# State space preparation in two feed forwards instead of three, modulation sums one stage later, low parts of weights back on VectorE

## The chip, the cores and the metric

The kernel runs on one core of one Trainium2 chip. The metric is the device time of one execution in microseconds (us). The profile is one execution of the same program, seen by the hardware profiler: TensorE (PE, with its weight loads as PEld), VectorE (DVE), ScalarE (ACT), GpSimd (POOL), and SyncE (SP), which issues the transfers.

## The reference, cut to what matters

Two blocks of two layers run one after the other on 256 latent rows and 256 context rows of width 1024. Every layer has a half feed forward, a mixer and another half feed forward, each one modulated by shift, scale and gate vectors that come from a condition vector. The mixers are a convolution module and a neighbourhood attention in the first block, a joint attention and an S5 state space mixer in the second.

```python
def second_block(x, c, ctx, c_ctx, mod_w, mod_b, ...):
    for l in range(DEPTH):
        m_lat = jnp.moveaxis((jax.nn.silu(c) @ mod_w[l] + mod_b[l]).reshape(b, N_MOD, 1, D_MODEL), 1, 0)
        h_lat = ffn_sublayer(h_lat, m_lat, 0, norm_pre[l, 0], norm_post[l, 0], ffn_w13[l, 0], ffn_w2[l, 0])
...
def s5_discretise(lam_re, lam_im, b_re, b_im, log_step):
    dt = jnp.exp(log_step)[:, None]
    mag = jnp.exp(lam_re * dt)
    a_re = mag * jnp.cos(lam_im * dt)
    a_im = mag * jnp.sin(lam_im * dt)
...
    bb_re = f_re[..., None] * b_re - f_im[..., None] * b_im
    bb_im = f_re[..., None] * b_im + f_im[..., None] * b_re
```

Nothing of `s5_discretise` depends on `x`, nor do the modulation vectors: both can be worked out at any time before their use. The outputs are float32.

## The kernel before, in words

**Matmuls.** All large products are made in pieces: each float32 operand is split into a high part, rounded for the matmul, and a low part, the rest. A product takes three matmuls (high by high, low by high, high by low). Activations lie transposed, 128 features on the partitions, in `hh` and `hl` (high and low): columns 0 to 255 are the latent stream, 256 to 511 the context stream.

**Weights.** `plan` lists all weight chunks in order. `pump` loads a chunk (`raw`, at most 1 MB, three buffers) from SP's queue, and for each piece of 8 tiles of 128 by 128 ScalarE writes the high part `wh` (L181) and another engine subtracts it for the low part `wl` (L186); five pieces are kept ahead. Which engine makes the low part is set by `cvm`: with 0 it is always VectorE, with 2 every second piece goes to GpSimd. `cvm` is 0 in the feed forwards with both streams (until the last products of one) and in the convolution, and 2 elsewhere. While `cv_behind` is set (during the convolution's layer norm) all go to GpSimd.

**Stages.** The order in time, with the names used here: f100, conv, f102, f110, na (neighbourhood attention), f112, f200, attn, f202, f210, s5, f212. A name f*bln* is the feed forward of block *b*, layer *l*, sublayer *n*. All run on both streams but f112 and f212, which have the latent one alone. A feed forward takes 22 gate and up tiles (`gu`) in three groups of 6, 8 and 8, and after each group the 8 down tiles (`pd`). Behind each `gu` pair VectorE multiplies (L778), ScalarE writes the high part `Hh` (L780), VectorE the low part `Hl` (L781).

**Side work.** The program is written in the order of TensorE's instructions, with a planner's clock `pe_t` that each matmul moves on by its cost (216 ns for 512 columns). A `Task` is a generator that takes a step whenever that clock passes its due time; a step that yields a number is followed by a pause of at least that many ns. Two tasks run inside the feed forwards. Each engine's own order follows from the program's order and from when the scheduler of the program takes an instruction to be ready.

- `mods` makes the modulation vectors on VectorE: each 128 of the 9216 outputs of a layer are one multiply and sum `jk` (L536) of a 512 KB weight tile `mw` with the condition vector, for one stream or both. Its period spreads the sums over 0.84 of a feed forward with both streams (0.8 of one with one stream). `open_mw` opens the buffers of `mw`, three by default.
- `s5_pre` works out the tables of the state space mixer. First constants on 64 columns (powers on GpSimd, sine and cosine on ScalarE, the rest on VectorE); then 8 groups, each with small powers on VectorE (`pn`, `pw`), `bb`, inputs `vw`, outputs `ow` and rotations `E` on GpSimd, 16 transposes `pvt` and 16 small products `kp` on TensorE, and transfers to DRAM (`dV`, `dO`, `dE`, `dK`). At the end of a group `toeplitz` reads `dK` back in a new order (`tt`) and stores `dT`. A step is due every 1500 ns (`PRE_STEP`). The task runs in f100, f102 and f110 and is drained after f110. All its buffers are in one pool, open from the start until after f110.

**Sums by stage before.** f100: 112 (from column group 16 on of layer (1,0), and the rest of that layer); f102: 48 of layer (1,1); f110: 64 of (1,1) and 48 of (2,0); f112: 48 of (2,0); f200: 48 of (2,0) and 48 of (2,1); f202: 64 of (2,1).

## Time and profile before

| | us |
|---|---|
| three runs, median | 3692.72 |
| three runs, lowest and highest | 3685.61 and 3693.66 |
| the profiled execution | 3693.2 |
| its span, first to last instruction | 3691.4 |
| TensorE matmuls, busy | 3497.5 (95% of the span) |
| TensorE weight loads, busy | 3058.1 (83%) |
| VectorE busy | 2641.6 (72%) |
| ScalarE busy | 1380.8 (37%) |
| GpSimd busy | 1199.6 (32%) |

Busy time is a mean over stages that differ, so the stages have to be read one by one. Matmuls are pipelined and their ends are modelled, so TensorE's busy time is not its peak rate. Times in the rows below count from the span's start.

### The profile page before, as it was taken

To read this page: it belongs to the slowest core of one execution; us is meant where nothing else is said; L and a number is where in the kernel's file an instruction comes from. 1 tells how busy PE (TensorE), PEld (TensorE's weight loads), DVE (VectorE), ACT (ScalarE), POOL (GpSimd) and SP (SyncE) were. 2 spreads that over 40 slices of the span, in tenths; PEclk is the share of its full clock that TensorE was granted. 3 is DMA by queue.
4 is the path that set the end of the run, shared out by engine and by line. 5 is a ranking of instruction groups with operands and counts; after the bars stand their busy time and mean duration, and the time that the engine had idled before them with its cause. 6 is when DMAs were issued, how large, how long until landed. Compare 5 with 4: busy or idle time off the path is not lost. (4 is left out here: it accounts for less than half of the span.)

```text
span 3691.4 us, 54762 instructions
## 1 busy us (share of the span) xinstructions
PE 3497.5 (95%) x21160; PEld 3058.1 (83%) x21160; DVE 2641.6 (72%) x4360; ACT 1380.8 (37%) x2430; POOL 1199.6 (32%) x1021
## 2 busy tenths in 40 slices
PE   8989999999999999999999998899999999997898
PEld 7768867988887788888998888778888988885898
DVE  8998798866589886778987766877565733368633
ACT  4222444422232223554343224555322432233443
POOL 5667301655564641123420004323000300035343
PEclk9999999999999999999999999999999999998899
DMA  7565311455447763235755542104455332238353
GB/s 255 174 219 201 131 69 41 166 171 186 158 147 261 266 212 123 101 115 184 258 197 198 183 145 93 45 31 142 166 198 172 139 113 103 92 115 286 123 186 126
DMA packets 158125, 580.41 MB, mean 157 GB/s; under 512 B 25252, under 2 KB 56740, under 8 KB 118184
## 3 DMA queue, kind: packets, MB, share of 16 engines
q1 hardware_dynamic: 157864, 576.91, 44.8%
q8 instruction: 166, 2.72, 0.3%
q14 instruction: 95, 0.78, 0.1%
HBM read 547.55 MB, written 29.29 MB: 156 GB/s over the span
## 5 line engine op out<-in xcount | busy, mean ns | idle before, releaser
L181 ACT ACTIVATE wh<-raw 128x1024 fp32r<-128x1024 f32 (+1 forms) x679 | 700.5, 1038 | 1353.3 <-PE gu L107 725.0
L107 PE MATMUL gu<-hl,wh 128*128 128x512 f32 (+1 forms) x3136 | 1084.0, 347 | 4.3 <-DVE hl L694 3.3
L107 PE MATMUL gu<-hh,wl 128*128 128x512 f32 (+1 forms) x3136 | 1082.5, 346 | 4.8 <-DVE wl L186 4.6
L107 PE MATMUL gu<-hh,wh 128*128 128x512 f32 (+1 forms) x3136 | 1078.4, 348 | 8.3 <-ACT hh L691 7.8
L186 DVE TENSOR_TENSOR wl<-raw,wh 128x1024 fp32r<-128x1024 f32 (+1 forms) x544 | 706.8, 1302 | 367.7 <-ACT wh L181 360.1
L186 POOL TENSOR_TENSOR wl<-raw,wh 128x1024 fp32r<-128x1024 f32 (+1 forms) x135 | 344.3, 2553 | 1278.4 <-ACT wh L181 1216.3
L536 DVE CUSTOM_DVE_ANT_0 jk<-mw,cb,vec 128x1024 bf16<-128x1024 f32 x480 | 704.8, 1468 | 50.8 <-DMA mw<-in_mw_dram 39.2
L107 PEld LDWEIGHTS gu<-hl,wh 128*128 128x128 f32 x3136 | 600.1, 191 | 77.6 <-DVE hl L694 4.8
L107 PEld LDWEIGHTS gu<-hh,wh 128*128 128x128 f32 x3136 | 597.5, 192 | 80.4 <-ACT hh L691 9.4
L107 PEld LDWEIGHTS gu<-hh,wl 128*128 128x128 f32 x3136 | 600.2, 192 | 76.9 <-DVE wl L186 5.9
L107 PE MATMUL pd<-Hh,wh 128*128 128x256 f32 (+1 forms) x1696 | 565.8, 335 | 19.3 <-ACT Hh L780 17.5
L107 PE MATMUL pd<-Hl,wh 128*128 128x256 f32 (+1 forms) x1696 | 567.8, 335 | 9.6 <-DVE Hl L781 9.6
L107 PE MATMUL pd<-Hh,wl 128*128 128x256 f32 (+1 forms) x1696 | 567.0, 335 | 0.0
L107 PEld LDWEIGHTS pd<-Hh,wh 128*128 128x128 f32 x1696 | 325.6, 192 | 52.9 <-ACT Hh L780 19.8
L107 PEld LDWEIGHTS pd<-Hl,wh 128*128 128x128 f32 x1696 | 326.2, 192 | 42.7 <-DVE Hl L781 11.7
L107 PEld LDWEIGHTS pd<-Hh,wl 128*128 128x128 f32 x1696 | 326.1, 192 | 30.4 <-issue 0.2
L778 DVE TENSOR_TENSOR gu<-sg,gu 128x512 f32<-128x512 f32 (+1 forms) x196 | 113.2, 578 | 203.6 <-PE gu L107 196.5
L107 PE MATMUL pj<-hh,wh 128*128 128x256 f32 (+1 forms) x736 | 226.5, 323 | 10.7 <-ACT hh L691 7.5
L107 PE MATMUL pj<-hl,wh 128*128 128x256 f32 (+1 forms) x736 | 227.7, 314 | 1.7 <-DVE hl L1089 1.0
L107 PE MATMUL pj<-hh,wl 128*128 128x256 f32 (+1 forms) x736 | 227.3, 314 | 0.8 <-DVE wl L186 0.8
L780 ACT ACTIVATE Hh<-gu 128x512 fp32r<-128x512 f32 (+1 forms) x196 | 98.6, 503 | 346.0 <-DVE gu L778 345.8
L107 PEld LDWEIGHTS pj<-hh,wh 128*128 128x128 f32 x736 | 142.5, 201 | 21.2 <-ACT hh L691 8.7
(403 smaller groups left out, 4602.0 us busy)
## 6 DMA issues: line engine op xcount, KB each, us to landing
raw<-in_gu_dram SPq DMA_DIRECT2D x186, 1024.0 KB, 4.8
mw<-in_mw_dram SPq DMA_DIRECT2D x280, 512.0 KB, 4.1
raw<-in_dn2b_dram SPq DMA_DIRECT2D x38, 1024.0 KB, 4.7
raw<-in_dn1b_dram SPq DMA_DIRECT2D x32, 1024.0 KB, 6.0
raw<-in_dn1a_dram SPq DMA_DIRECT2D x16, 768.0 KB, 4.4
raw<-in_pw_dram SPq DMA_DIRECT2D x12, 1024.0 KB, 4.8
raw<-in_dn2a_dram SPq DMA_DIRECT2D x16, 768.0 KB, 4.2
dO<-ow SPq DMA_DIRECT2D x32, 256.0 KB, 2.7
```

Source lines behind the costliest of these rows:

```text
L107: ins = self.last_mm = self.nc.tensor.matmul(out=out, lhsT=lhsT, rhs=rhs, start=start, stop=stop, **kw)
L181: ins = nc.scalar.activation(out=h2, in_=r, func=AF.Copy)
L186: self.low_p = lambda eng=eng, l2=l2, r=r, h2=h2: eng.tensor_sub(l2, r, h2.bitcast(F32))
L536: self.behind_pe(nc.vector.tensor_tensor_reduce(out=jk, in0=tl[i], in1=self.cb[s], scale=1.0, scalar=self.V(f"mod_b{b}{l}")[:, j:j + 1], o ...
L778: nc.vector.tensor_mul(pr[:, :n], sg[:, :n], pu[:, :n])
L780: nc.scalar.activation(out=hi, in_=pr[:, :n], func=AF.Copy)
```

## The change: what it does

- `s5_pre` takes a pause of its own after the constants (`yield "pause"`: the task is taken off the list). It starts again in f102, and only then is the pool for the buffers of the groups opened (`s5w`, through `work`). The 8 groups run in f102 and f110.
- `toeplitz` of a group no longer follows it with pauses of 4000 and 5000 ns: it is kept as `back`, and its four chunks are issued one by one between the parts of the next group (`next(back, None)`). Only behind the last group it runs by itself. Both halves share one buffer `tt`.
- The modulation sums of (2,0) column group 0 move from f110 to f112, those of group 1 from f112 to f200, those of (2,1) group 0 from f200 to f202. In f112 they come ahead of the norm of the context stream (`ctx_norm`). f110 no longer loads the second block's condition vectors. Sums by stage: f100 112, f102 48, f110 64, f112 48, f200 96, f202 112.
- f102 and f110 have two `mw` buffers instead of three.
- `cvm` is gone: low parts of weights are made on VectorE everywhere, but for the time in which `cv_behind` is set.

```diff
@@ -69,7 +69,9 @@
     def step(self):
         r = next(self.gen, "end")
         self.done = r == "end"
-        if not self.done:
+        if r == "pause":
+            self.k.stop(self)
+        elif not self.done:
             self.t = max(self.t + self.period, self.k.pe_t + max(r or 0, 0.5 * self.period))
 
 
@@ -82,7 +84,7 @@
         self.chains = []
         self.ticking = False
         self.tasks = []
-        self.cvm, self.cv_behind = 2, None
+        self.cv_behind = None
         P = lambda name, bufs, **kw: ctx.enter_context(tc.tile_pool(name=name, bufs=bufs, **kw))
         self.pool = lambda name, bufs=1, side="left": tc.tile_pool(name=name, bufs=bufs, side=side, reuse_waits="tile")
         self.const = P("const", 1)
@@ -181,7 +183,7 @@
             ins = nc.scalar.activation(out=h2, in_=r, func=AF.Copy)
             if self.cv_behind:
                 self.behind(ins, self.cv_behind)
-            eng = nc.gpsimd if (self.cvm and self.n_cv % self.cvm == 1) or self.cv_behind else nc.vector
+            eng = nc.gpsimd if self.cv_behind else nc.vector
             self.low()
             self.low_p = lambda eng=eng, l2=l2, r=r, h2=h2: eng.tensor_sub(l2, r, h2.bitcast(F32))
             self.cv_t[self.n_cv] = (hi, lo)
@@ -719,7 +721,6 @@
         nc, tc = self.nc, self.tc
         two = len(streams) == 2
         N = 512 if two else T
-        self.cvm = 0 if two else 2
         with ExitStack() as es:
             Hh = Hl = fp = None
 
@@ -855,7 +856,6 @@
                         self.drain(task)
                     if side is not None:
                         self.stop(side)
-                    self.cvm = 2
                 if full < KT:
                     ws = {}
                     for s in streams:
@@ -1092,7 +1092,6 @@
                 self.rstd(ch, acc, 2, 1e-5, apply, d1=0, d2=0)
                 rdy[s] = ch
 
-            self.cvm = 0
             w0 = [self.take() for _ in range(2)]
             for s in S2:
                 self.force(ready[s])
@@ -1131,7 +1130,6 @@
             self.release(2 * L)
             go()
             self.cv_behind = None
-            self.cvm = 2
             mean(KT - 1, CTX)
             layernorm(CTX)
             self.cv_behind = None
@@ -1855,7 +1853,7 @@
         self.dT = [t(f"dT{d}", [128, 1024]) for d in range(8)]
         self.dU = [t(f"dU{d}", [128, 512]) for d in range(8)]
 
-    def s5_pre(self, sp):
+    def s5_pre(self, sp, work):
 
         nc = self.nc
         g, v, a = nc.gpsimd, nc.vector, nc.scalar
@@ -1944,6 +1942,8 @@
         v.tensor_mul(fi, fi, den)
         yield
         three = lambda t: t.rearrange("p (d q) -> p d q", d=2)
+        yield "pause"
+        sp = work()
         bbz = [sp.tile([128, 2, 4, 32], F32, name=f"bbz{i}") for i in range(2)]
         for t in bbz:
             g.memset(t, 0.0)
@@ -1965,15 +1965,16 @@
         def toeplitz(d):
 
             for hf in range(2):
-                tt = sp.tile([128, 4, 128], F32, tag=f"vt{hf}", name="tt")
+                tt = sp.tile([128, 4, 128], F32, tag="tt", name="tt")
                 src = self.dK[d].rearrange("(g h) e -> h g e", h=16)
                 for j in range(8):
                     nc.sync.dma_start(out=tt[16 * j:16 * j + 16], in_=src[:, 4 * hf:4 * hf + 4, 16 * j:16 * j + 128])
-                yield 5000
+                yield
                 nc.sync.dma_start(out=self.dT[d][:, 512 * hf:512 * hf + 512].rearrange("p (g e) -> p g e", g=4), in_=tt)
-                yield 4000
+                yield
 
         ahead = load(0)
+        back = iter(())
         for d in range(8):
             bc = ahead
             if d < 7:
@@ -2130,11 +2131,15 @@
                                           in_=t[:, 4 * r:4 * r + 4, :].rearrange("p q e -> p (q e)"))
 
 
+            next(back, None)
             V1 = yield from inputs(1)
+            next(back, None)
             O1 = yield from outputs(1)
             yield from turned(1, V1)
+            next(back, None)
             V0 = yield from inputs(0, lambda: store_outputs(1, O1))
             yield from steps(1, O1)
+            next(back, None)
             O0 = yield from outputs(0)
             yield from turned(0, V0)
             E = yield from rotations()
@@ -2142,8 +2147,10 @@
             yield from steps(0, O0)
             store_rotations(E)
             nc.sync.dma_start(out=self.dK[d], in_=kt)
-            yield 4000
-            yield from toeplitz(d)
+            back = toeplitz(d)
+        yield 4000
+        for _ in back:
+            yield 5000
 
     def plan_s5(self):
         for p in range(4):
@@ -2389,8 +2396,8 @@
         self.plan_s5()
         self.plan_ffn(2, 1, 1)
 
-        with self.pool("s5p", 1, "right") as sp:
-            pre = Task(self, self.s5_pre(sp), PRE_STEP)
+        with self.pool("s5p", 1, "right") as sp, ExitStack() as late:
+            pre = Task(self, self.s5_pre(sp, lambda: late.enter_context(self.pool("s5w", 1, "right"))), PRE_STEP)
             self.open_mw(None)
             begin = self.begin
             self.mark("f100")
@@ -2401,20 +2408,15 @@
             self.close_mw()
             self.mark("conv")
             self.conv(ready, gates(1, 0, 1), lambda s, acc: norm(1, 0, 2, s, acc))
-            self.open_mw(["c", "c_ctx"])
+            self.open_mw(["c", "c_ctx"], 2)
             self.mark("f102")
             self.ffn(1, S2, ready, gates(1, 0, 2), lambda s, acc: norm(1, 1, 0, s, acc),
                      work=self.mods(mods(1, 1, [0], 40)), side=pre, **ht("102"))
             self.close_mw()
-            self.open_mw(["c", "c_ctx"])
+            self.open_mw(["c", "c_ctx"], 2)
             self.mark("f110")
-
-            def two_mods():
-                yield from self.mods(mods(1, 1, [1, 2], 40))[0]
-                self.c_names = ["c_2", "c_ctx_2"]
-                yield from self.mods(mods(2, 0, [0]))[0]
             self.ffn(1, S2, ready, gates(1, 1, 0), lambda s, acc: norm(1, 1, 1, s, acc),
-                     work=(two_mods(), 116), side=pre, **ht("110"))
+                     work=self.mods(mods(1, 1, [1, 2], 40)), side=pre, **ht("110"))
             self.close_mw()
             self.drain(pre)
         self.mark("na")
@@ -2454,23 +2456,23 @@
         self.mark("f112")
 
         def norm_and_mods():
+            yield from self.mods(mods(2, 0, [0]))[0]
             yield from ctx_norm()
-            yield from self.mods(mods(2, 0, [1]))[0]
-        self.ffn(1, (LAT,), ready, gates(1, 1, 2, (LAT,)), final, work=(norm_and_mods(), 58))
+        self.ffn(1, (LAT,), ready, gates(1, 1, 2, (LAT,)), final, work=(norm_and_mods(), 61))
         self.close_mw()
 
         self.open_y()
         self.open_mw(["c_2", "c_ctx_2"])
         self.mark("f200")
         self.ffn(2, (CTX, LAT), ready, gates(2, 0, 0), after2(2, 0, 0, (2, 0, 1)),
-                 work=self.mods(mods(2, 0, [2]) + mods(2, 1, [0])), **ht("00"))
+                 work=self.mods(mods(2, 0, [1, 2])), **ht("00"))
         self.close_mw()
         self.mark("attn")
         self.attn2(ready, after2(2, 0, 1, (2, 0, 2)))
         self.open_mw(["c_2", "c_ctx_2"])
         self.mark("f202")
         self.ffn(2, S2, ready, gates(2, 0, 2), after2(2, 0, 2, (2, 1, 0)),
-                 work=self.mods(mods(2, 1, [1, 2], 40)), **ht("02"))
+                 work=self.mods(mods(2, 1, [0]) + mods(2, 1, [1, 2], 40)), **ht("02"))
         self.close_mw()
         tabs = self.es.enter_context(self.pool("s5t"))
         self.s5_tab = {}
```

## Rows read from the trace of the kernel before

**Rows 1.** The page: busy time of each engine, share of the span, instructions.

```profile
PE 3497.5 (95%) x21160; PEld 3058.1 (83%) x21160; DVE 2641.6 (72%) x4360; ACT 1380.8 (37%) x2430; POOL 1199.6 (32%) x1021
```

**Rows 2.** Windows by stage: us; PE, PEld, DVE, ACT, POOL busy (count); clock; DMA.

```profile
29.60:438.00 408.40, 389.88 (x1886) 323.93 (x1887) 371.27 (x633) 117.22 (x176) 266.91 (x221) 0.98 0.58 198
669.00:1050.00 381.00, 378.52 (x2053) 323.31 (x2052) 264.48 (x413) 123.00 (x185) 215.10 (x233) 1.00 0.49 166
1050.00:1451.00 401.00, 382.66 (x2006) 324.66 (x2005) 322.72 (x459) 117.87 (x175) 197.07 (x200) 0.97 0.62 213
...
1671.00:1881.00 210.00, 200.50 (x1589) 197.76 (x1590) 190.86 (x244) 93.05 (x144) 93.07 (x35) 0.96 0.62 226
1881.00:2262.00 381.00, 372.79 (x2006) 324.84 (x2004) 276.83 (x424) 124.13 (x188) 28.43 (x21) 0.98 0.49 172
2530.00:2908.00 378.00, 371.90 (x1996) 323.97 (x1996) 238.91 (x366) 127.14 (x196) 32.73 (x26) 0.99 0.48 165
```

**Rows 3.** Waits of TensorE in f100: us in total, times, longest.

```profile
PE pd L107 <- ACT Hh L780: 7.5, 2, 4.9
PE pd L107 <- DVE Hl L781: 6.8, 3, 3.3
PE pvt L107 <- POOL vw L2034: 2.7, 1, 2.7
```

**Rows 4.** Waits of TensorE in f110.

```profile
PE pvt L107 <- POOL vw L2026: 8.1, 1, 8.1
PE pd L107 <- ACT Hh L780: 4.6, 2, 3.8
PE pd L107 <- DVE Hl L781: 2.6, 2, 1.8
PE gu L107 <- DVE wl L186: 2.6, 1, 2.6
```

**Rows 5.** Windows around a stall of f100 and one of f110.

```profile
239.00:270.00 31.00, 17.53 (x55) 13.05 (x56) 28.03 (x41) 5.68 (x7) 14.22 (x7) 0.78 0.65 223
1097.00:1117.00 20.00, 11.47 (x62) 10.23 (x63) 17.75 (x21) 4.05 (x7) 19.86 (x12) 0.74 0.76 218
```

**Rows 6.** Timeline at the end of na: start, us, engine, line, operation.

```profile
1650.56 5.80 POOL L186 TENSOR_TENSOR wl<-raw,wh 128x1024 fp32r<-128x1024 f32 x2 [0.44 <-ACT wh L181]
...
1651.46 5.18 DVE L1223 TENSOR_TENSOR x<-x,t 128x256 f32<-128x256 f32 x2
```

**Rows 7.** Groups of VectorE's instructions in f100: busy us, mean ns, idle before.

```profile
L536 DVE CUSTOM_DVE_ANT_0 jk<-mw,cb,vec 128x1024 bf16<-128x1024 f32 x112 | 170.0, 1518 | 10.3 <-DMA mw<-in_mw_dram 9.7
```

**Rows 8.** Groups of VectorE's instructions in f110.

```profile
L536 DVE CUSTOM_DVE_ANT_0 jk<-mw,cb,vec 128x1024 bf16<-128x1024 f32 x112 | 161.3, 1440 | 38.7 <-DMA mw<-in_mw_dram 29.5 <-ACT cb L507 7.8
```

**Rows 9.** Groups of VectorE's instructions in f112.

```profile
L536 DVE CUSTOM_DVE_ANT_0 jk<-mw,cb,vec 128x1024 bf16<-128x1024 f32 x48 | 93.1, 1940 | 0.4
L186 DVE TENSOR_TENSOR wl<-raw,wh 128x1024 fp32r<-128x1024 f32 x29 | 43.2, 1490 | 1.8 <-ACT wh L181 1.7
L293 DVE TENSOR_TENSOR acc<-acc,sq 128x256 f32<-128x256 f32 x13 | 16.6, 1278 | 2.9 <-ACT sq L283 2.9
```

**Rows 10.** Groups of VectorE's instructions in f200.

```profile
L536 DVE CUSTOM_DVE_ANT_0 jk<-mw,cb,vec 128x1024 bf16<-128x1024 f32 x96 | 122.8, 1279 | 0.8
L186 DVE TENSOR_TENSOR wl<-raw,wh 128x1024 fp32r<-128x1024 f32 x63 | 79.2, 1260 | 35.8 <-ACT wh L181 34.0
```

**Rows 11.** Timeline of GpSimd in f102; in brackets its idle time before.

```profile
776.73 1.23 POOL L2022 TENSOR_TENSOR vw<-pw,bb 128x512 f32<-128x512 f32 x1 [27.82 <-PE pvt L107]
...
793.74 1.18 POOL L2059 TENSOR_TENSOR ow<-pw,bc 128x576 f32<-128x576 f32 x1 [9.04 <-PE kp L107]
```

**Rows 12.** Waits of TensorE in f112.

```profile
PE pd L107 <- ACT Hh L780: 5.4, 3, 2.7
```

**Rows 13.** Waits of TensorE over the whole span.

```profile
PE ssq L107 <- DVE acc L293: 15.3, 3, 7.9
PE ssq L107 <- DVE acc L1469: 14.4, 6, 5.9
```

## Prediction

> **What bounds the kernel now.** The profiled execution took 3693.2 us, its span is 3691.4 us, and the median of the three runs is 3692.72 us; the sum below is made against 3693.2 us. Under 0.2% (7.4 us) a measurement of this kernel can't be told from no change. I read the page first: TensorE is busy for 3497.5 us of the span [rows 1], so what a change can give back is the 194 us in which it idles and what it loses at the lower clock. None of the edits takes a matmul away. Then the windows by stage [rows 2]: two feed forwards with both streams and about 2,000 matmuls take 378 and 381 us (f202, f200), but the one called f110 takes 401 us, and f100 takes 408 us for 1886. VectorE is the most loaded other engine there (371 us of 408 in f100, 323 of 401 in f110, 191 of 210 in f112).
>
> Then who TensorE waits for. In f100: 14.3 us for the split of the last gate products (ScalarE's `Hh`, VectorE's `Hl`, both behind VectorE's queue) and 2.7 us for GpSimd's `vw` [rows 3]. In f110: 8.1 us for `vw`, 7.2 us for the split, 2.6 us for a weight's low part [rows 4]. In f102, with the same state space work but 48 modulation sums, TensorE is busy for 378.5 of 381 us [rows 2]. So these stages lose where VectorE's and GpSimd's loads meet. The windows around the stalls show 0.78 and 0.74 of the full clock [rows 5], so part of them runs at the lower of TensorE's two levels (1.2 against 2.4 GHz), after TensorE had stood still.
>
> Why the two loads meet: at the end of na two low parts run on GpSimd for 5.80 us, and in the same stretch two additions on VectorE take 5.18 us together, where the next one takes 0.41 us [rows 6]. A VectorE instruction with two operands in SBUF stands still while GpSimd works. The sums `jk` show it in the mean: 1279 ns in f200, where GpSimd is idle, 1518 ns in f100, 1440 ns in f110, 1940 ns in f112 [rows 7 to 10].
>
> **The change, part by part.**
>
> *State space work leaves f100.* Everything after the constants (8 column groups) now starts in f102. By the planner's arithmetic (a step each 1.5 us of its clock, 58 steps and 22 us of pauses a group before), f100 held about 2.5 groups, f102 3.1, f110 2.4; their transposes and products are moved, not saved. In f100 112 sums at 1518 instead of 1279 ns are 27 us of VectorE, the groups' own small operations some 20 us more; 371 us fall to about 320 of 390. f200 with 277 us of VectorE loses nothing inside. The price f100 pays now: 14.3 + 2.7 us of waits, and in the 31 us window a lost 0.22 of the clock, 6.8 us, of which 57% lies on matmuls (17.53 of 31 us busy): 3.9 us. Together 21 us. The 112 sums stay, so some rest: **-18 us** (bounds -21 and -8).
>
> *Denser groups in f102 and f110.* A group now takes 53 steps, 82 us of the planner's clock plus 5 us for its own matmuls; the pauses of 22 us behind each group go, since the chunks of `toeplitz` ride between the next group's steps. 8 groups fill the two feed forwards almost exactly; by the arithmetic only the last group's rotations, its 8 small products and its `dK`, `dT` transfers are left for the drain behind f110. What covers the density: in f102 GpSimd waits 27.82 us for the `pvt` transposes and 9.04 us for `kp` in each group [rows 11]. Of those 37 us the removed pauses take 23 (22 at 381 us for the planner's 360), 14 stay. Behind TensorE's `pvt` stand all later matmuls; behind GpSimd's lateness stand the `dV` and `dO` stores on SP, and behind them weights and `mw`. I take **+2 us** (0 to +15, two waits like f110's 8.1 us). The drain's DMAs, four steps on SP in a row, meet three raw weight buffers that are already loaded: nothing, at most 5 us, in the same bound.
>
> *Sums one stage on, buffers from 3 to 2.* f110 goes from 112 to 64 sums: 48 x 1.44 = 69 us of VectorE leave it, while the denser groups add some 40 us of small operations and blocking: 323 us become about 295 of 383. Its price now: 8.1 + 4.6 + 2.6 + 2.6 = 17.9 us of waits [rows 4] and at 0.74 of the clock over 20 us with 11.47 busy 3.0 us more [rows 5], a like stretch at 1266 us 2 us: 23 us, which is also 401 less f202's 378 us for the same number of matmuls [rows 2]. I take **-18 us** (-23 to 0). The second `mw` buffer less gives a sum two periods of 4.5 us from the freed buffer to its use, where f110 before had three of 2.5 us and waited 29.5 us [rows 8]; hidden.
>
> f202 goes from 64 to 112 sums, 48 x 1.28 = 61 us: VectorE from 239 to 300 of 378 us, over f200's 277 which waits for nothing inside, at the pace of 2.57 us a sum that f110 had; half of the sums of the last part use a buffer once only. Below: nothing. Above: all that f110 paid, 23 us. It is nearer to f200, since GpSimd's 33 us do not block it: **+5 us**. f200 keeps 96 sums.
>
> f112 keeps 48 sums, of an earlier group, and the context norm moves behind them; its chain has the last fifth of the stage, some 35 us, as cover, against some 15 us of work. Nothing.
>
> *No low parts on GpSimd.* 135 of them took 344.3 us there; on VectorE 135 x 1.26 = 170 us [rows 10]. Most fall where VectorE has room. The tight stage is f112: 33 low parts x 1.26 = +42 us. Against it: 48 sums fall from 1940 to 1279 ns (-32 us), 29 low parts from 1490 to 1260 (-7 us), 13 additions from 1278 to about 700 (-7 us): -46 us [rows 9, 10]. So VectorE's load stays near 187 us, but no instruction waits behind a 2.5 us one. f112's waits are 5.4 us for `Hh` [rows 12] and 3.5 us for others; I take **-6 us** (-9 to +22).
>
> The Trainium skill speaks against this edit: Perfetto Trace Analysis, section Optimizing Scalar/DVE Operations, says that where VectorE is saturated, handing some work to GpSimd may make sense (and adds that the shared port may undo it). By that rule alone f112 would have 191 + 42 = 233 us of VectorE and grow by some 22 us; by the rows it shrinks by 6.
>
> The ends of na, attn, s5 and of the feed forwards: TensorE waits 15.3 us for the additions of L293 and 14.4 us for those of L1469 before the norms [rows 13], the longest 7.9 us at na's end, where the blocked additions of [rows 6] stand just before. With low parts of 1.26 us on VectorE's own queue I take half of these 29.7 us: **-14 us** (-28 to +5).
>
> Sum: -18 + 2 - 18 + 5 - 6 - 14 = -49 us, 3693.2 - 49 = **3644 us**.
>
> **The rivals.**
> 1. *GpSimd's chain is too long in f102 and f110* (the other side). For it: its operations take up to 2.2 us where others are done in 1.3, and the pauses that let it catch up are gone. Against: the 14 us of slack. If blocking lengthens each group by more than that, TensorE waits at `pvt` in each of 8 groups as in f110, 8.1 + 3.0 us: +88 us, 3732 us. It turns the sign from five such waits on (55 us). Chance 0.08.
> 2. *f202 takes over f110's stalls*: same 112 sums, same pace: +23 instead of +5, 3662 us. Against: GpSimd is quiet there. 0.15.
> 3. *f112 bound by VectorE*, if the blocked time does not come back with the low parts: +22 instead of -6, 3672 us. For: VectorE at 191 of 210 us. 0.10.
> 4. *f100's stalls come from its 112 sums, not from the groups*: only GpSimd's 2.7 us and the clock behind it go: -6 instead of -18, 3656 us. For: VectorE's queue, not GpSimd, is what the matmuls wait for. 0.12.
> 5. *The change only moves the waits*: each stall returns in the stage that took the work; within 7 us of 3693. 0.07.
> My forecast has the remaining 0.48.
>
> **How the numbers follow.** The forecast and rivals 2, 3 and 4 are faster: 0.85. Rival 5 is the same: 0.07. Rival 1 is slower: 0.08. The low end adds the lower bounds that can fall together: -21 - 23 - 9 - 28 = -81, 3612 us. The high end leaves out rival 1 and most of rival 5: 3690 us.
>
> **What would show it.** f100 from 29.6 us on at about 390 us with TensorE waiting for `Hl` hardly at all, its GpSimd quiet after the constants, `jk` there near 1300 ns. f102 and f110 both near 383 us, GpSimd at some 270 us in each, and few waits at `pvt`. f112 near 204 us, with `jk` at 1280 ns. No GpSimd row at L186 outside conv's end; the `ssq` waits halved. Wrong it would be if `pvt` waits appear in every group, if f202 passes 390 us, or if f112 grows.

## The result and the profile after

The changed kernel takes 3631.97 us (median of 4 runs, 3627.7 to 3638.44), the kernel before in the same comparison 3690.14 us (4 runs, 3685.61 to 3693.66): a ratio of 0.9846 with a 95% interval of 0.9834 to 0.9859. The forecast was 3644 us with a range of 3612 to 3690 us. The profiled execution took 3634.95 us, its span is 3633.2 us, 58.2 us less than before.

The page of the changed kernel, its line of busy time, beside that of before [rows 1]:

```profile
PE 3480.3 (96%) x21160; PEld 3051.0 (84%) x21160; DVE 2600.0 (72%) x4493; ACT 1386.4 (38%) x2428; POOL 769.7 (21%) x888
```

The same matmuls, 17 us less busy time, so a better clock; the other 41 us are idle time that is gone. GpSimd lost 430 us of work and VectorE still is no busier.

To see where it came from I cut both traces at the first matmul of each stage. All stage lengths in this text are such differences, each from one profiled execution:

```
us       f100   conv   f102   f110     na   f112   f200   attn   f202   f210     s5   f212
before  408.8  230.6  380.7  401.6  219.6  210.6  380.6  268.2  378.1  378.4  199.9  204.7
after   375.8  233.1  391.2  387.5  217.9  192.7  376.3  267.7  378.4  376.1  201.9  205.1
        -33.0   +2.5  +10.5  -14.1   -1.7  -17.9   -4.3   -0.5   +0.3   -2.3   +2.0   +0.4
```

They are good to some 4 or 5 us: f110 took 387.5 us here and 383.5 us in a later kernel that has the same f110. In the changed kernel and the seven made from it that leave attn and f202 as they are, attn took 262.4 to 267.7 us. f202 is steadier there, with 378.4 to 379.9 us. The windows of the changed kernel at these cuts (f100, f102, f110, f112, f200, f202), columns as in [rows 2]:

```profile
29.40:405.20 375.80, 374.78 (x1786) 315.58 (x1787) 310.99 (x579) 113.30 (x162) 57.62 (x48) 1.00 0.54 189
...
638.30:1029.40 391.10, 383.74 (x2065) 327.31 (x2065) 280.26 (x437) 125.95 (x188) 265.66 (x311) 0.98 0.50 168
1029.40:1416.90 387.50, 383.81 (x2099) 326.44 (x2097) 270.53 (x396) 122.02 (x183) 243.69 (x292) 0.99 0.60 201
...
1634.80:1827.50 192.70, 192.66 (x1592) 192.66 (x1593) 175.18 (x278) 94.57 (x144) 1.68 (x1) 0.99 0.68 241
1827.50:2203.80 376.30, 370.27 (x2002) 322.71 (x2000) 274.12 (x429) 124.33 (x188) 12.04 (x14) 1.00 0.50 173
...
2471.60:2850.00 378.40, 371.38 (x1996) 323.80 (x1996) 298.12 (x470) 127.73 (x194) 20.29 (x20) 0.99 0.57 200
```

The windows of before at these cuts, f100 and f112:

```profile
29.60:438.40 408.80, 390.28 (x1889) 324.33 (x1890) 371.67 (x633) 117.39 (x176) 267.31 (x221) 0.98 0.58 197
...
1670.90:1881.50 210.60, 201.10 (x1593) 198.36 (x1594) 191.46 (x244) 93.15 (x144) 93.57 (x35) 0.96 0.62 225
```

In f100 and f112 TensorE now hardly stands still (374.78 of 375.80 and 192.66 of 192.70 us busy), at 1.00 and 0.99 of the clock. f110 comes close, with VectorE at 271 of 388 us instead of 323 of 401. f102 is the one that got worse: 7 us idle, and 0.98 of the clock where before it had 1.00.

Groups of VectorE's instructions in the changed kernel: `jk` in f100, then the low parts and `jk` in f112 (columns as in [rows 7, 9]):

```profile
L538 DVE CUSTOM_DVE_ANT_0 jk<-mw,cb,vec 128x1024 bf16<-128x1024 f32 x112 | 143.1, 1278 | 0.5
...
L188 DVE TENSOR_TENSOR wl<-raw,wh 128x1024 fp32r<-128x1024 f32 x59 | 71.6, 1219 | 8.6 <-ACT wh L183 8.2
L538 DVE CUSTOM_DVE_ANT_0 jk<-mw,cb,vec 128x1024 bf16<-128x1024 f32 x48 | 61.3, 1277 | 0.6 <-ACT cb L509 0.5
```

The sum that took 1518 ns in f100 and 1940 ns in f112 takes 1278 and 1277 ns where GpSimd is quiet. In f102 and f110, where the groups run, it still takes 1558 and 1486 ns. What TensorE waits for now, in f102 (two lines), in f110 (two lines) and over the whole span (two lines, against [rows 13]):

```profile
PE gu L109 <- DVE hl L696: 3.7, 3, 2.5
PE ssq L109 <- DVE acc L295: 3.2, 1, 3.2
...
PE gu L109 <- DVE Hl L782: 2.0, 1, 2.0
PE pd L109 <- DVE Hl L782: 1.2, 1, 1.2
...
PE ssq L109 <- DVE acc L295: 14.4, 4, 4.9
PE ssq L109 <- DVE acc L1467: 9.2, 3, 3.7
```

No wait for `vw` is left in either stage. The waits of f102 all lie in its first 20 us. Windows around the old stall of f100 [rows 5] and over the new one at the start of f102:

```profile
239.00:270.00 31.00, 31.00 (x139) 25.67 (x138) 26.67 (x43) 7.32 (x7) 0.00 (x0) 1.00 0.52 187
638.30:660.00 21.70, 14.34 (x81) 13.08 (x81) 21.49 (x27) 11.88 (x21) 18.39 (x20) 0.74 0.42 119
```

In the second one VectorE is busy for 21.49 of 21.70 us and GpSimd for 18.39. The timelines of VectorE and of GpSimd there:

```profile
637.69 2.47 DVE L696 SCALAR_TENSOR_TENSOR hl<-nt,mod,hh 128x256 fp32r<-128x256 f32 x3
...
643.32 2.77 DVE L696 SCALAR_TENSOR_TENSOR hl<-nt,mod,hh 128x256 fp32r<-128x256 f32 x3
...
650.24 2.51 DVE L1146 TENSOR_TENSOR x<-x,t 128x256 f32<-128x256 f32 x3
652.67 3.78 DVE L295 TENSOR_TENSOR acc<-acc,sq 128x256 f32<-128x256 f32 x3
...
636.57 1.47 POOL L1952 TENSOR_TENSOR pt<-bc,cfr 128x128 f32<-128x128 f32 x1 [4.49 <-DMA bc<-in_s5bc_dram]
...
653.63 1.24 POOL L2031 TENSOR_TENSOR vw<-pw,bb 128x512 f32<-128x512 f32 x1
```

GpSimd's first group begins just where VectorE makes the norm on which the first matmuls of f102 wait, and from there on GpSimd hardly pauses.

### The profile page after: what moved, and what is told of

Read it like the earlier page. It is cut to its first block, busy times and chain, and to the rows that moved or that the text cites. A ratio compares the mean times of both kernels' runs of the same rounds, so it can differ in the third digit from the quotient of the medians.

```text
span 3633.2 us, 54649 instructions
## 1 busy us (share of the span) xinstructions
PE 3480.3 (96%) x21160; PEld 3051.0 (84%) x21160; DVE 2600.0 (72%) x4493; ACT 1386.4 (38%) x2428; POOL 769.7 (21%) x888
## 4 chain that ended last, share of the span: by engine, by line
PE 87%; DVE 8%; ACT 2%; POOL 1%; issue 1%; DMA 0%; SPq 0%; POOLq 0%; DVEq 0%; ACTq 0%
PE gu L109 46%; PE pd L109 23%; PE pj L109 8%; PE po L109 2%; PE ptap L109 1%; PE pv L109 1%; PE pk L109 1%; PE ps L109 1%; DVE wl L188 1%; PE bc L109 1%; PE pq L109 1%; PE pT L109 1%; PE ssq L109 0%; DVE ry L2239 0%; DVE tl L1538 0%
## 5 line engine op out<-in xcount | busy, mean ns | idle before, releaser
L188 DVE TENSOR_TENSOR wl<-raw,wh 128x1024 fp32r<-128x1024 f32 (+1 forms) x677 | 841.2, 1247 | 365.9 <-ACT wh L183 352.7
L538 DVE CUSTOM_DVE_ANT_0 jk<-mw,cb,vec 128x1024 bf16<-128x1024 f32 x480 | 640.5, 1334 | 71.2 <-DMA mw<-in_mw_dram 66.7
L268 POOL TENSOR_TENSOR rr<-rv,mhalf 128x2 f32<-128x2 f32 (+1 forms) x37 | 33.4, 903 | 1930.5 <-DVE rv L266 1917.1
L109 PEld LDWEIGHTS pj<-hh,wh 128*128 128x128 f32 x736 | 142.4, 201 | 23.8 <-ACT hh L693 10.0
L109 PEld LDWEIGHTS pj<-hl,wh 128*128 128x128 f32 x736 | 145.9, 199 | 9.4 <-issue 1.7
```

The costliest lines, as they stand in the source:

```text
L109: ins = self.last_mm = self.nc.tensor.matmul(out=out, lhsT=lhsT, rhs=rhs, start=start, stop=stop, **kw)
L188: self.low_p = lambda eng=eng, l2=l2, r=r, h2=h2: eng.tensor_sub(l2, r, h2.bitcast(F32))
L268: nc.gpsimd.tensor_tensor(r[:, :ncol], v[:, :ncol], self.mhalf[:, :ncol], ALU.pow)
L538: self.behind_pe(nc.vector.tensor_tensor_reduce(out=jk, in0=tl[i], in1=self.cb[s], scale=1.0, scalar=self.V(f"mod_b{b}{l}")[:, j:j + 1], o ...
```

## The experiments

My theory after the result: each of the three parts acts in its own stage and by one mechanism, VectorE instructions with two operands in SBUF that are held up while GpSimd reads. The rivals: the parts need each other; GpSimd's work as such, not its reading, is what costs; f102 pays for the moved matmuls rather than for its start.

### Each part alone, and the whole without one

**Low parts alone**, on the kernel before:

```diff
-            eng = nc.gpsimd if (self.cvm and self.n_cv % self.cvm == 1) or self.cv_behind else nc.vector
+            eng = nc.gpsimd if self.cv_behind else nc.vector
```

> The kernel before with one edit: low parts of weights on VectorE everywhere but in the convolution's layer norm. Theory (GpSimd's low parts blocked VectorE, and that was all of f112's loss): f112 falls from 210.6 to 193 us, the ends of stages give 5 us, f100 and f110 stay at 409 and 402 us; about 3667 us in all. Rival (f112 gained in the changed kernel because its sums now come first and the context norm last): f112 stays above 205 us, about 3685 us. Rival from the prediction (VectorE becomes f112's bound): f112 above 220 us, about 3705 us.

3674.69 us against 3691.41, ratio 0.9956 (0.9940 to 0.9973): -16.7 us. f112 goes from 210.6 to 193.7 us, as the theory said, but the whole missed it by 7.7 us. Most of that lies in f110: it takes 409.1 us instead of 401.6, and TensorE is idle there for 21.9 instead of 18.3 us:

```profile
1051.50:1460.60 409.10, 387.20 (x2010) 328.63 (x2009) 313.73 (x462) 118.28 (x175) 180.78 (x197) 0.97 0.61 209
```

Why this stage, which still has both loads, stalls for longer was not found. Against it, na, attn, f202 and f210 are shorter by 2.5, 5.2, 2.5 and 2.2 us (attn within its own scatter). The VectorE groups of f112 are those of the changed kernel:

```profile
L186 DVE TENSOR_TENSOR wl<-raw,wh 128x1024 fp32r<-128x1024 f32 x58 | 70.3, 1217 | 9.9 <-ACT wh L181 9.9
L536 DVE CUSTOM_DVE_ANT_0 jk<-mw,cb,vec 128x1024 bf16<-128x1024 f32 x48 | 61.2, 1275 | 0.1
```

**Sums alone**, with the two `mw` buffers, on the kernel before:

```diff
...
-                     work=(two_mods(), 116), side=pre, **ht("110"))
+                     work=self.mods(mods(1, 1, [1, 2], 40)), side=pre, **ht("110"))
...
+            yield from self.mods(mods(2, 0, [0]))[0]
             yield from ctx_norm()
-            yield from self.mods(mods(2, 0, [1]))[0]
...
-                 work=self.mods(mods(2, 1, [1, 2], 40)), **ht("02"))
+                 work=self.mods(mods(2, 1, [0]) + mods(2, 1, [1, 2], 40)), **ht("02"))
```

> The kernel before with the modulation sums one stage later and two instead of three sum buffers in f102 and f110, nothing else. Theory: f110, with 64 sums for 112, falls from 401.6 to about 380 us; f202, with 112 for 64, stays at 378 us since GpSimd is quiet there; f112 stays near 210 us; about 3669 us in all. Rival (f110's stalls come from GpSimd's groups, whatever the sums): f110 stays above 395 us, about 3688 us. Rival (f202 takes the stalls over): f202 at 395 us or more, about 3685 us.

3664.64 us, ratio 0.9928 (0.9913 to 0.9943): -26.8 us. f110 falls from 401.6 to 374.7 us, further than the 380 expected. Its window and the only wait of TensorE in it that is listed:

```profile
1050.00:1424.80 374.80, 374.39 (x2011) 320.31 (x2010) 256.18 (x359) 118.13 (x173) 169.04 (x200) 1.00 0.56 193
```

```profile
PE gu L107 <- DVE hl L694: 0.4, 1, 0.4
```

The state space work is that of before (200 instructions of GpSimd), and the stalls are gone, the wait for `vw` among them, at the full clock. GpSimd takes 169 us for it, where before it took 198 us. One sum still takes 1493 ns here, so this stage did not lose its stalls by quicker sums: VectorE has 256 us to do instead of 323. f202, which took the sums, goes from 378.1 to 382.6 us, where the theory had it unchanged:

```profile
2496.60:2879.20 382.60, 374.25 (x1997) 326.27 (x1997) 300.32 (x466) 127.56 (x196) 33.22 (x26) 0.98 0.56 197
```

f112 goes from 210.6 to 206.0 us though its low parts are as before: its sums now come ahead of the context norm, and some 4 us go with that order.

**Groups alone** (the pause, the late pool and `toeplitz` between the steps of the next group), on the kernel before:

```diff
...
+        yield "pause"
+        sp = work()
...
-            yield 4000
-            yield from toeplitz(d)
+            back = toeplitz(d)
...
```

> The kernel before with the state space groups in f102 and f110 alone (late pool, interleaved dK and dT transfers), sums and low parts as before. Theory (stalls come where a stage has both 112 sums and groups): f100 falls from 409 to about 376 us (10 us of it are matmuls that move), f102 grows to about 391 us, f110, with 112 sums and nearly twice the groups, grows by 15 us or more to 417 us or more; the whole within 12 us of 3690. Rival (the groups alone set the stalls, and packing them costs nothing): f110 at 410 us or less, of which 8 us are moved matmuls, about 3672 us.

3675.15 us, ratio 0.9962 (0.9947 to 0.9977): -16.3 us. f100 goes from 408.8 to 375.3 us with its 112 sums, f102 from 380.7 to 390.2 us. f110 with 112 sums and 4 groups instead of 2.5 takes 410.5 us, 8.9 more than before, of which some 5 us are moved matmuls (worked out below). Waits of TensorE there:

```profile
PE pd L109 <- ACT Hh L782: 10.1, 2, 6.1
PE pd L109 <- DVE Hl L783: 4.1, 2, 2.9
PE gu L109 <- DVE Hl L783: 3.9, 3, 2.7
PE gu L109 <- DVE wl L188: 3.0, 1, 3.0
```

21.5 us where before had 18.3 in such a list. I had expected 417 us or more; the rival's 410 us came out. A stage with 112 sums and no groups (f100 here) does not stall, nor does one with groups and 64 sums (f110 of the sums alone). It is 112 sums and groups in one stage that stall.

**The whole without its low parts** (GpSimd makes every second one again):

```diff
...
-            eng = nc.gpsimd if self.cv_behind else nc.vector
+            eng = nc.gpsimd if (self.cvm and self.n_cv % self.cvm == 1) or self.cv_behind else nc.vector
...
```

> The changed kernel with every second low part of the one-stream and mixer stages on GpSimd again, as before. Theory: f112 goes back from 192.7 to about 210 us, the ends of stages lose 5 us, the feed forwards with two streams stay; about 3655 us. Rival (f112's gain came with the order of its sums): f112 stays near 195 us, about 3638 us.

3653.9 us, ratio 0.9899 (0.9885 to 0.9914): 21.9 us slower than the changed kernel, as the theory said. f112 is back at 206.5 us (206.0 with the sums alone), 13.8 above the changed kernel; f200, f202, f210 and na are longer by 5.6, 3.5, 5.8 and 3.7 us, conv and s5 shorter by 3.3 and 3.9. VectorE's and GpSimd's groups in f112:

```profile
L538 DVE CUSTOM_DVE_ANT_0 jk<-mw,cb,vec 128x1024 bf16<-128x1024 f32 x48 | 89.1, 1855 | 0.8 <-ACT cb L509 0.5
L188 DVE TENSOR_TENSOR wl<-raw,wh 128x1024 fp32r<-128x1024 f32 x29 | 45.4, 1565 | 2.9 <-ACT wh L183 2.9
...
L188 POOL TENSOR_TENSOR wl<-raw,wh 128x1024 fp32r<-128x1024 f32 x30 | 87.2, 2908 | 99.9 <-ACT wh L183 89.5 <-DVE hl L696 4.2 <-PE bc L109 3.2
```

The three parts alone give -16.7 - 26.8 - 16.3 = -59.8 us, the whole -58.2. They add up within their intervals (some 5 us each): in the total no part needs another. Stage by stage they don't quite: f200 lost 4.3 us in the whole, and 0.8 us at most in any part alone.

### What of GpSimd's work costs: reading or working

Both kernels are the changed one with work of GpSimd added beside every second piece of f112's weights (the first pieces are made while na ends), on scratch tiles that nothing else uses. The first only writes:

```diff
+            if self.scr and self.n_cv % 2 == 1:
+                t = self.scr.tile([128, 1024], F32, tag="scr", name="scr")
+                nc.scalar.activation(out=t[:, 0:1], in_=r[:, 0:1], func=AF.Copy)
+                for j in range(2):
+                    nc.gpsimd.memset(t, float(j))
...
```

> The changed kernel with idle work for GpSimd in f112: beside every second piece two fills of a scratch tile, some 2 us, which write SBUF and read nothing; a ScalarE copy of one column makes them wait for the piece. All low parts stay on VectorE. Theory (VectorE is held up by GpSimd's reading of SBUF, not by GpSimd being busy): jk stays near 1300 ns and f112 at 192 to 196 us. Rival (any GpSimd instruction of that length holds VectorE up, or disturbs the stage by its waits): jk near 1900 ns, f112 205 us or more.

3628.27 us, ratio 0.9827 (0.9808 to 0.9847); f112 192.8 us. Groups of f112:

```profile
L193 DVE TENSOR_TENSOR wl<-raw,wh 128x1024 fp32r<-128x1024 f32 x59 | 71.6, 1221 | 8.2 <-ACT wh L183 8.0
L543 DVE CUSTOM_DVE_ANT_0 jk<-mw,cb,vec 128x1024 bf16<-128x1024 f32 x48 | 61.4, 1279 | 1.2 <-ACT cb L514 1.1
...
L188 POOL MEMSET scr<- 128x1024 f32 x62 | 59.2, 954 | 128.7 <-ACT scr L186 127.0
```

The second reads two tiles:

```diff
+                nc.gpsimd.tensor_tensor(t, self.scro, self.scro, ALU.add)
...
```

> The same, but the idle work of GpSimd beside every second piece is one addition of two tiles in SBUF, 128 by 1024, as long as a low part. Theory (reading SBUF on GpSimd holds up VectorE's instructions with two SBUF operands): jk near 1900 ns as before the change, and since VectorE now makes all low parts as well, f112 at 215 us or more. Rival (the loss of f112 before came from the late low parts of GpSimd, which TensorE waited for): jk near 1300 ns, f112 below 200 us.

3660.12 us, ratio 0.9914 (0.9894 to 0.9933); f112 219.9 us. Groups of f112, its window, TensorE's two longest kinds of waits in it, and its waits for `acc`, one ahead of the stage (9.9 us) and one near its end:

```profile
L542 DVE CUSTOM_DVE_ANT_0 jk<-mw,cb,vec 128x1024 bf16<-128x1024 f32 x48 | 76.7, 1598 | 0.6 <-ACT cb L513 0.5
L192 DVE TENSOR_TENSOR wl<-raw,wh 128x1024 fp32r<-128x1024 f32 x58 | 87.9, 1523 | 3.1 <-ACT wh L183 3.1
...
L187 POOL TENSOR_TENSOR scr<-scro 128x1024 f32<-128x1024 f32 x31 | 70.3, 2269 | 143.0 <-ACT scr L186 143.0
```

```profile
1637.80:1857.70 219.90, 204.15 (x1593) 201.19 (x1594) 215.14 (x274) 97.27 (x174) 71.89 (x32) 0.95 0.59 207
...
PE gu L109 <- DVE Hl L786: 4.0, 3, 1.8
PE pd L109 <- ACT Hh L785: 3.7, 2, 2.8
...
PE ssq L109 <- DVE acc L299: 12.0, 2, 9.9
```

59 us of writing cost nothing, 70 us of reading cost 27 us of the stage: it is the reading that costs, on data that has nothing to do with the matmuls. VectorE is busy for 215 of 220 us. The sum `jk` slowed to 1598 ns and not to the 1900 that I expected. The wait of 9.9 us lies at the end of na, where three of the additions run; it is 4.9 us in the changed kernel and 4.8 us in the one that only writes. Two things limit this. The two kernels differ also in the length of one instruction of GpSimd (0.95 against 2.27 us). And the test was made in f112 alone: in f100 and f110 the groups also bring small operations to VectorE, and no run separates these from the blocking.

### The start of f102

The first group starts 15 us later, its steps come each 1.4 instead of 1.5 us so that the groups end in time:

```diff
-PRE_STEP = 1500
+PRE_STEP = 1400
...
         yield "pause"
+        yield 15000
         sp = work()
```

> The changed kernel with the groups started 15 us of the planner's clock later in f102 and a step due each 1400 instead of 1500 ns, so that they still end within f110. Theory (f102's 10 us more are 4 us of moved matmuls and a start in which GpSimd's first group holds up the norm that TensorE waits for): f102 falls from 391 to about 384 us, and na by 2 us since less is left for the drain; f110 as it is; about 3623 us. Rival (f102 lost to the density of the groups, not to its start): f102 stays at 391 us or grows, f110 grows too; 3632 us or more.

3623.5 us, ratio 0.9819 (0.9802 to 0.9835), 8.5 us below the changed kernel. f102 takes 383.3 us, at the full clock, with GpSimd busier than in the changed kernel (window of f102; then two rows of VectorE's timeline at its start, which answer to the first and the last VectorE row of the changed kernel):

```profile
637.80:1021.10 383.30, 380.99 (x2082) 324.61 (x2081) 281.76 (x437) 125.38 (x189) 284.02 (x322) 1.00 0.53 177
```

```profile
637.24 1.27 DVE L696 SCALAR_TENSOR_TENSOR hl<-nt,mod,hh 128x256 fp32r<-128x256 f32 x3
...
645.45 1.48 DVE L295 TENSOR_TENSOR acc<-acc,sq 128x256 f32<-128x256 f32 x3
```

The three `hl` take 1.27 instead of 2.47 us, the additions 1.48 instead of 3.78. GpSimd works more in this f102 and not less, so it was the start that cost, and not the density of the groups.

### The pauses, the buffers, the convolution

**Pauses kept:** the changed kernel, with `toeplitz` behind its own group as before.

```diff
...
-            back = toeplitz(d)
+            yield 4000
+            for _ in toeplitz(d):
+                yield 4500
```

> The changed kernel with the transfers of dK and dT behind each group again, with 22 us of the planner's pauses. By the planner's arithmetic 114 steps, two groups, are then left for the drain behind f110. Theory: TensorE waits there for two groups of GpSimd's work, some 2 x 65 us less what is taken ahead; na starts 60 to 120 us later, about 3700 to 3750 us in all, and that is what the interleaving of these transfers is for. Rival (the scheduler takes GpSimd's work ahead as long as buffers allow, so little is left): less than 30 us.

3678.23 us, ratio 0.9958 (0.9943 to 0.9973), 46.3 us above the changed kernel. The theory had 60 to 120 us, the rival less than 30; it lies between. f110 falls by 11.5 to 376.0 us, but the stage of na goes from 217.9 to 276.9: what didn't fit is drained there. TensorE's longest waits in that stage, and its window:

```profile
PE pvt L109 <- POOL vw L2026: 29.0, 2, 26.9
PE pvt L109 <- POOL vw L2034: 6.3, 2, 4.9
```

```profile
1404.50:1681.40 276.90, 220.58 (x1508) 198.11 (x1505) 166.10 (x415) 127.11 (x302) 75.28 (x126) 0.88 0.37 121
```

**Three `mw` buffers** in f102 and f110 of the changed kernel:

```diff
-            self.open_mw(["c", "c_ctx"], 2)
+            self.open_mw(["c", "c_ctx"])
...
```

> The changed kernel with three instead of two buffers for the weights of the sums in f102 and f110. Theory (two periods of 4.5 us or more cover a transfer): no difference that can be measured, 3632 us within 5 us, jk's waits for mw in f110 some us less. Rival (two buffers make VectorE wait and through it TensorE): f102 and f110 together 5 us or more shorter, 3627 us or less.

3630.28 us (3628.24 to 3638.52), ratio 0.9839 (0.9820 to 0.9857): no difference from the changed kernel. VectorE's waits for `mw` in f110 fall from 54.9 to 28.0 us, and TensorE's only listed wait in f110 is 2.0 us, which the changed kernel has too. f102 and f110 together take 773.7 instead of 778.7 us, but the convolution's kernel below, with two buffers, has 773.6: that is scatter.

**The convolution's low parts** behind its layer norm on VectorE as well, in the changed kernel:

```diff
-            eng = nc.gpsimd if self.cv_behind else nc.vector
+            eng = nc.vector
```

> The changed kernel with the low parts made during the convolution's layer norm on VectorE as well, so none are left on GpSimd. Theory (GpSimd's low parts hold VectorE up at the end of each stage): conv falls by 2 to 4 us from 233 us, about 3629 us. Rival (VectorE is what the layer norm waits for, and more work on it is worse than waiting behind GpSimd): conv grows by 2 us or more, 3634 us or more.

3629.17 us (3623.97 to 3631.29), ratio 0.9829 (0.9810 to 0.9848); the stage takes 231.7 instead of 233.1 us. Not to be told from no change.

**Late start and convolution together:**

> The changed kernel with two edits together: the first group starts 15 us later in f102 (and its steps come each 1.4 us instead of 1.5), and the convolution's low parts behind its layer norm go to VectorE too. My theory: the two edits touch different stages, so the late start gives its 8.5 us (f102 at 383 us, f110 at 384 to 388) and the conv edit the 0 to 3 us that it measured by itself (conv stage at 231 to 233 us): 3618 to 3624 us. The rival, that the 8.5 us of the late start were a variation between executions (f110 has come out at 383.5 and at 387.9 us in kernels that have the same f110): 3628 to 3633 us, with f102 at 390 us again.

3621.32 us (3620.37 to 3623.14, 5 runs), ratio 0.9808 (0.9795 to 0.9822). f102 at 383.8 us, conv at 228.9 us: the late start's gain is no variation between executions, and this is the fastest version of the study, 10.7 us below the changed kernel.

## Why the prediction held, and where its terms were off

**f100, -18 us: right in kind, too small.** The stage lost 33.0 us, but not all is gain. The state space matmuls that left it took 6.51 us (40 `pvt`) and 2.67 us (64 `kp`) in the trace of before, together 9.2 us. So 23.8 us are stalls and clock, above even the bound of 21. TensorE's idle time fell from 18.5 to 1.0 us: these 17.5 us are the waits that I had listed (17.0), and nearly all went, where I had left some to rest. The term that was mis-sized is the clock: I counted the lower clock over the 31 us around the stalls (3.9 us), where the whole stage ran at 0.98 [rows 2]. The matmuls that stayed took 390.3 - 9.2 = 381.1 us before and 374.8 now, 6.3 us less. Rival 4 is refuted: the 112 sums stayed and not one gap of 0.8 us is left inside f100.

**f102, +2 us: the step that failed.** It grew by 10.5 us, of which 2.4 are 16 moved `pvt`. I looked at how much slack GpSimd has in the middle of a group [rows 11] and found enough, rightly: no `pvt` waits appeared, and rival 1 is dead. I didn't ask where the first group begins. At 636 us it meets VectorE's norm chain, for which TensorE waits. The 8 us that this costs lie within the range that I gave (0 to 15), but in another place; with the late start 383.3 us are left, which is 380.7 and the moved matmuls.

**f110, -18 us: right.** It fell by 14.1 us, though 24 `pvt` (2.9 us) and 64 `kp` (2.0 us) came in; without these 4.9 us it is -19.0. The sums did it: alone they are worth 26.9 us in this stage, while the groups alone lengthen it by 8.9 (4.9 of it those matmuls). VectorE came to 271 us, not to 295: from the 256 us of the sums alone the denser groups added some 14 us, not 40. That the second `mw` buffer less is hidden holds (three buffers change nothing).

**f202, +5 us: right, though the stage shows +0.3.** Two terms cancel here. The sums alone lengthened f202 by 4.5 us (378.1 to 382.6); with the low parts gone too it is back at 378.4, and the low parts alone shorten it by 2.5. In the two kernels without GpSimd's low parts it takes 375.6 us with 64 sums and 378.4 with 112. VectorE is busy for 298 us, as worked out. Rival 2 (+23 us) is refuted.

**f112, -6 us: right in kind, a third of its size.** The stage lost 17.9 us in the whole change; the low parts alone are worth 16.9 us on the kernel before and 13.8 in the changed one, and the order of the sums some 4 us, which I had put at nothing. Before, TensorE was idle for 9.5 us of the stage (201.10 of 210.6 us busy), now for none: that is little more than the 8.9 us of waits that I had listed. The other 8.4 us are a term that I left out. The same matmuls take 192.66 instead of 201.10 us, and most of that is the clock, 0.96 before and 0.99 now: 201.10 x 0.96 is 193.1 and 192.66 x 0.99 is 190.7. The 0.96 stood in the window that I quoted [rows 2]. VectorE's load fell to 175 us, not 187: the additions fell to 417 ns, not to 700, the low parts added 31 us, not 35, and smaller instructions gave back 3 us. I had written that such VectorE instructions stand still while GpSimd works; the kernel with `memset` shows that work which only writes does not hold them up. Rival 3 is refuted. So is, for this stage, the hand-over to GpSimd that the Trainium skill suggests for a saturated VectorE (Perfetto Trace Analysis, section Optimizing Scalar/DVE Operations); the doubt that it adds in the next sentence is what the runs show: with half of the low parts on GpSimd the stage takes 206.5 us, with none 192.7.

**The ends, -14 us: right in kind, too large.** The `ssq` waits [rows 13] fell from 29.7 to 14.4 + 9.2 = 23.6 us, not to half. The stages that hold them beside no other term (conv, na, f200, attn, f210, s5, f212) lost 3.9 us together, and f202 some 4.1 behind its sums (382.6 to 378.4 us): some 8 us, with a scatter of stages of the same size. At na's end 7.9 us became 4.9: the blocked additions explain 3 us, and the 4.9 us that are left stand where GpSimd is at rest, so its low parts are not their cause. In exchange the drain's transfers now stand on SP ahead of the first loads of na. There `pv` waits for `vt` for 2.4 us, once; that the transfers are the cause is not shown.

**The sum.** In place of -18 + 2 - 18 the three feed forwards gave -36.6 us with the matmuls moved among them; f202's sums +4.4, f112 -17.9, the ends -8.0: -58.1 us against -49. The 9 us between come from f112 (-12) and the three feed forwards (-2.6), less what the ends did not give (+6). So the nearness of the total is in part luck: f112 was too small and the ends too large, and f102's 8 us stand against a larger gain in f100.

**What I said would show it** was right for `jk` (1278 and 1277 ns), for GpSimd in f102 (266 us), and for the absence of `pvt` waits. It was wrong for f100 (390 us, and it took 376), since there I left the moved matmuls in and too much of the clock out, for f102 at 383 us (391), for f112 at 204 us (193) and for the halved `ssq` waits. f110, at 387.5 us for 383, is within the scatter.

**What stays open.** In the late start and in the fastest version f110 has one stall of 6.2 us at a `pd` that waits for `Hl`, which the changed kernel does not have; I did not follow it. Nor did I separate the drain's transfers on SP from the rest of na, or find why the low parts alone lengthen f110 by 7.5 us.

## What to carry to other kernels

Two loads that each fit can stall TensorE where they meet; here it was enough to take one of them, or 48 of 112 sums, to another stage. When a stage is costed, count the granted clock of the whole stage beside the waits: in f112 it was worth nearly as much. And when background work of GpSimd is moved, ask what VectorE does in the microseconds in which it starts: a start at a norm chain cost 8 us here, and a start 15 us later gave them back.

## What the runs showed of the hardware

In f112 work of GpSimd slowed VectorE where it read SBUF and not where it only wrote. 62 `memset` of 954 ns left `jk` at 1279 ns and the low parts at 1221 ns; 31 additions of two tiles in SBUF raised them to 1598 and 1523 ns. These two groups alone lost 48 x 0.32 + 58 x 0.30 = 33 us of VectorE to 70 us of GpSimd, and the stage grew by 27 us. The Trainium skill (SBUF — State Buffer, section Who interferes with whom) says that a VectorE instruction with two inputs in SBUF contends with a GpSimd instruction that reads SBUF and not with one that only writes it; the traces of f112 agree, and show it for the multiply and sum `jk` as well as for plain subtractions.

```profile
L186 POOL TENSOR_TENSOR wl<-raw,wh 128x1024 fp32r<-128x1024 f32 x30 | 85.3, 2844 | 103.9 <-ACT wh L181 87.3 <-PE gu L107 11.3 <-DVE G L661 2.8
```

The same low part takes 2844 ns on GpSimd beside a busy VectorE in f112 of the kernel before (row above) and 1219 ns on VectorE in the changed kernel, so each one that is handed over there costs GpSimd more than twice what it saves VectorE, before VectorE's own loss is counted. GpSimd loses too: its 200 instructions in f110 took 198 us beside 112 sums and 169 us beside 64.

A few hundredths of the granted clock weigh nearly as much as the waits: in f112, at 0.96 over 210 us, TensorE's matmuls took 8.4 us longer than at 0.99 now, beside 9.5 us in which it stood idle.
